# A hybrid streaming encoder layer: the top-k search of ten row tiles made in five pairs

## The chip, the core and the metric

The kernel runs on one core of one Trainium2 chip. The metric is the device time of one execution in microseconds (us). Five engines work from queues of their own, each in the order in which the program was written out: TensorE (PE for its matmuls, PEld for its weight loads), VectorE (DVE), ScalarE (ACT), GpSimd (POOL), and SyncE (SP), which issues nearly all DMAs.

## The reference, cut to what matters

One layer mixes three groups of heads: a gated delta rule with a short convolution (A), sparse attention (B) and attention over 256 memory tokens (C). All read one input projection `h @ w_in`. The change lies in group B, where an indexer scores every key for every query, and the keys of the 256 largest scores are kept:

```
adm = (k_pos[None, :] // CHUNK) <= (q_pos[:, None] // CHUNK)
logits = jnp.einsum('bqhd,bsd->bqhs', qi, ki)
score = jnp.einsum('bqh,bqhs->bqs', wi, jax.nn.relu(logits))
score = jnp.where(adm[None], score, -jnp.inf)
_, idx = lax.top_k(score, n_sel)        # n_sel = 256
```

There are 2048 prompt tokens (16 tiles of 128 rows, g = 1 to 16) and 128 sample tokens (tile 0, with 4112 keys each from a cache). Tile g of the prompt has 128 g keys, so tiles 1 and 2 keep all of them and tiles 3 to 16 search.

## The kernel before, in words

The kernel does not sort. For a tile of 128 queries it finds a threshold per row: `topk` takes mean and variance of a quarter of the scores (bn_stats on every fourth column), guesses the threshold T from a normal quantile, and corrects it in up to six counts (`NIT = 6`). A count is one pass of ScalarE over the scores, a sign with bias -T whose accumulator gives the number of keys above T; a chain of small instructions on VectorE then keeps the bracket (a lower and an upper point with their counts, in st4) and computes the next T. One pass of relu, fused multiply and max finds the scores next to the last T, the exact threshold is picked among them by rank, and a last pass writes a bias of 0 or -2**100 per key, which attention adds later. The count of the last pass must come out at 256: the square of its error is added to fail, and at the program's end a nonzero fail starts a slow exact selection.

In each small instruction of a search 128 rows of one tile lie on the partitions and one or two columns on the free axis: T, f (the count less 256), the masks, the bracket.

The program has two parts, each a set of generators that `weave` runs by modelled times: it takes the generator whose time is smallest, lets it issue one step and puts that step's modelled cost on its engine. What the engines run is the order that comes out of this and of the scheduler that follows it. In the first part (to about 1500 us) the generators are: the projections of five groups of row tiles (4, 4, 3, 3 and 3 tiles) with three matmuls per product of split operands (pp); their preparation; three stages of the delta rule (pa, pb, pl, po; GpSimd computes Lm for its block inverse, VectorE solves Xs step by step); and the index: memory keys, the sample tile, then `idx_prompt` for tiles 3 to 13 one after the other. Per tile, `idx_prompt` waits until the keys of the tile are projected (`done["i"] > g`), loads and splits the queries (`q_stack`: qr, qn, qst), computes 8 heads x ceil(W/512) matmuls into two PSUM buffers (pi), takes relu on ScalarE and adds the weighted result to score on VectorE, lets GpSimd set the masked corner of score, and runs `topk`. score has one buffer, so a tile's scoring starts when the search before is through. Tiles 14 to 16 follow in the second part (attention and output).

The names in rows: score is the tile of scores, junk the sign's output, tf holds f, T, f and -T, st is st4, msk the masks, tmp scratch, sg, thr and cnt the sign, threshold and counts, mv, sd, sdr, t_b the mean, the deviation and its inverse root. pp, pi, pa, pb, pl, po are PSUM tiles.

Weights come in by `load_w`, three raw pieces (wr) at a time, only in the first group; wh and wl are their split halves, kept in DRAM for the later groups.

Of the kernel before, what the change touches and what calls it, by code (L numbers as in the profile page):

```python
# [5 lines left out]
F32 = mybir.dt.float32  # L6
# [13 lines left out]
NT = 17  # L20
# [186 lines left out]
def build(tc, nc, a):  # L207
# [41 lines left out]
    fail = cpool.tile([128, 1], F32, name="fail")  # L249
# [207 lines left out]
    def idx_post(gi, t0, m, raw, sm, final):  # L457
# [3 lines left out]
        sq = spool.tile([128, 2, 32], F32, name="isq")  # L461
# [64 lines left out]
    def topk(pieces, get, put, g, tp):  # L526


        W = sum(w for _, w in pieces)
        ti = g - 2 if g else 15  # L530
        wst = 4096 if g == 0 else W - 128
        st = tp.tile([128, 8, 6], F32, name="bst")
        n = 0
        turn = [1]

        def order_():
            turn[0] = -turn[0]
            return range(len(pieces))[::-turn[0]]
        for i in order_():
            c0, w = pieces[i]  # L540
            s = yield from get(i)
            hi = min(w, wst - c0)
            for lo in range(0, hi, 2048):
                V.bn_stats(st[:, n, :], s[:, lo:min(lo + 2048, hi):4])
                n += 1
            put(i, -turn[0])
            yield 1
        mv = tp.tile([128, 2], F32, name="mv")
        V.bn_aggr(mv, st[:, :n, :])
        sd = tp.tile([128, 1], F32, name="sd")  # L550
        V.tensor_scalar(sd, mv[:, 1:2], 1e-30, None, op0=OP.add)
        rs = tp.tile([128, 1], F32, name="sdr")
        rsqrt(rs, sd, tp, "t")
        V.tensor_tensor(sd, sd, rs, op=OP.mult)
        zc = C("zc")[:, 2 * ti:2 * ti + 2]
        st4 = tp.tile([128, 4], F32, name="st4")
        V.scalar_tensor_tensor(st4[:, 0:1], sd, -4.0, mv[:, 0:1], op0=OP.mult, op1=OP.add)
        V.scalar_tensor_tensor(st4[:, 2:3], sd, 6.0, mv[:, 0:1], op0=OP.mult, op1=OP.add)
        V.memset(st4[:, 1:2], -float(NSEL))
        V.memset(st4[:, 3:4], float(W - NSEL))  # L560
        tf = tp.tile([128, 4], F32, name="tf")
        V.scalar_tensor_tensor(tf[:, 1:2], sd, zc[:, 0:1], mv[:, 0:1], op0=OP.mult, op1=OP.add)
        slope = tp.tile([128, 1], F32, name="slope")
        V.tensor_tensor(slope, sd, zc[:, 1:2], op=OP.mult)
        cnt = tp.tile([128, 4], F32, name="cnt")
        tmp = tp.tile([128, 4], F32, name="tmp4")
        msk = tp.tile([128, 4], I32, name="msk")

        def total():
            if len(pieces) > 1:  # L570
                V.tensor_reduce(cnt[:, 3:4], cnt[:, :len(pieces)], axis=AX.X, op=OP.add)
                return cnt[:, 3:4]
            return cnt[:, 0:1]

        def count():
            V.tensor_scalar(tf[:, 3:4], tf[:, 1:2], -1.0, None, op0=OP.mult)
            for i in order_():
# [3 lines left out]
                S.activation(jk[:, :w], s, AF.Sign, bias=tf[:, 3:4], accum_out=cnt[:, i:i + 1])  # L581
                put(i, -turn[0])
                yield 1
            V.tensor_scalar(tf[:, 0::2][:, :2], total().to_broadcast([128, 2]), 0.5, W / 2.0 - NSEL,
                            op0=OP.mult, op1=OP.add)
# [3 lines left out]
        for it in range(NIT):  # L589
            yield from count()  # L590
            if it == NIT - 1:
                break
            f, t_ = tf[:, 0:1], tf[:, 1:2]
            V.tensor_scalar(msk[:, 0:1], f, 0.0, None, op0=OP.is_gt)
            V.tensor_scalar(msk[:, 1:2], f, 0.0, None, op0=OP.is_le)
            V.copy_predicated(st4[:, 0:4:3], msk[:, 0:1].to_broadcast([128, 2]), tf[:, 1:3])
            V.copy_predicated(st4[:, 1:3], msk[:, 1:2].to_broadcast([128, 2]), tf[:, 0:2])
            V.tensor_tensor(tmp[:, 0:1], f, f, op=OP.mult)
            V.tensor_scalar(msk[:, 2:3], tmp[:, 0:1], 56.0 if it < 4 else 230.0, None, op0=OP.is_gt)
            if it == 0:  # L600
                V.scalar_tensor_tensor(tmp[:, 1:2], f, slope, t_, op0=OP.mult, op1=OP.add)
            else:
                V.tensor_tensor(tmp[:, 2:4], st4[:, 2:4], st4[:, 0:2], op=OP.subtract)
                V.reciprocal(tmp[:, 3:4], tmp[:, 3:4])
                V.scalar_tensor_tensor(tmp[:, 1:2], tmp[:, 3:4], st4[:, 3:4], tmp[:, 2:3], op0=OP.mult, op1=OP.mult)
                V.tensor_tensor(tmp[:, 1:2], tmp[:, 1:2], st4[:, 0:1], op=OP.add)
            V.copy_predicated(t_, msk[:, 2:3], tmp[:, 1:2])
            yield 1
# [26 lines left out]
        for i in range(3):  # L635
            if i:
                V.match_replace(tv, tops[:, 8 * i - 8:8 * i], tv, -3e38)
# [1315 lines left out]
```

## Time and profile before

| what | value |
|---|---|
| median of 3 runs | 2352.61 us (2351.39 to 2356.84) |
| profiled execution, its own time | 2355.36 us |
| its span, first to last instruction | 2353.5 us |
| mean granted TensorE clock | 0.946 |
| busy: TensorE, weight loads | 2096.8 us (89%), 1645.1 us (70%) |
| busy: VectorE, ScalarE, GpSimd | 1651.6 us (70%), 1292.9 us (55%), 419.7 us (18%) |

An engine's busy time counts its instructions alone; a matmul's end is modelled, so a busy TensorE can still be held up a little. A granted clock of 1 is 2.4 GHz, 0.5 is 1.2 GHz. Idle time in front of an instruction is put down to what it waited for last.

### The profile page before, as it was taken

The numbers are of one execution on the slowest core, as the hardware profiler recorded it, in microseconds if no ns is written. First come the engines' busy times: TensorE is split into PE (matmuls) and PEld (weight loads), VectorE is DVE, ScalarE is ACT, GpSimd is POOL, SyncE is SP. The second block draws the span as 40 slices with busy tenths as digits, with TensorE's granted clock in tenths as the row PEclk, the third lists the DMA queues.
The fourth block names the chain that finished last, engine by engine and source line by source line (L and its number), as shares of the span: only waits on it lengthen the run. The fifth ranks groups of instructions, "written<-read, shape, count | busy, mean of one in ns | idle before, by whom it ended". The sixth has DMA issues, their size and how long they took to land.

```text
span 2353.5 us, 43495 instructions
## 1 busy us (share of the span) xinstructions
PE 2096.8 (89%) x14123; PEld 1645.1 (70%) x14123; DVE 1651.6 (70%) x6571; ACT 1292.9 (55%) x3193; POOL 419.7 (18%) x494
## 2 busy tenths in 40 slices
PE   4887989788899998999899999989999999799997
PEld 3755645677688887888788888756566555467665
DVE  4765655566888787899888996777567667554552
ACT  3454545455546565676666764467456656544552
POOL 3231413211121111111111021132111111111100
PEclk9887989788999998999899999999999999999998
DMA  7688667765544555656555555368788777653212
GB/s 230 177 242 224 214 147 212 196 233 192 198 159 161 183 176 197 206 196 218 181 204 203 198 202 201 117 211 262 246 249 272 246 238 249 189 165 101 91 48 69
DMA packets 323533, 453.25 MB, mean 193 GB/s; under 512 B 81760, under 2 KB 230880, under 8 KB 303840
## 3 DMA queue, kind: packets, MB, share of 16 engines
q1 hardware_dynamic: 322976, 449.32, 59.9%
q8 instruction: 114, 1.87, 0.3%
q0 software_dynamic: 320, 1.06, 0.2%
q14 instruction: 123, 1.01, 0.1%
HBM read 344.53 MB, written 105.75 MB: 191 GB/s over the span
## 4 chain that ended last, share of the span: by engine, by line


## 5 line engine op out<-in xcount | busy, mean ns | idle before, releaser
L169 PE MATMUL pp<-wh,xh 128*128 128x256 f32 (+1 forms) x952 | 290.0, 305 | 10.6 <-ACT v L169 4.5
L169 PE MATMUL pp<-wh,xl 128*128 128x256 f32 (+1 forms) x952 | 280.6, 295 | 1.5 <-DVE xl L169 1.4
L169 PE MATMUL pp<-wl,xh 128*128 128x256 f32 (+1 forms) x952 | 280.5, 295 | 1.3 <-POOL wl L169 1.2
L169 PE MATMUL pp<-xh,wh 128*128 128x384 f32 (+1 forms) x640 | 249.5, 390 | 5.6 <-ACT q L169 3.2
L169 ACT ACTIVATE relu<-pi 128x512 f32<-128x512 f32 (+3 forms) x340 | 183.4, 545 | 125.0 <-PE pi L169 67.1
L169 PE MATMUL pp<-xh,wl 128*128 128x384 f32 (+1 forms) x640 | 242.2, 379 | 2.3 <-DMA wl<-wd2l 1.7
L169 DVE SCALAR_TENSOR_TENSOR score<-relu,w,score 128x512 f32<-128x512 f32 (+3 forms) x304 | 221.7, 731 | 29.5 <-ACT relu L169 15.0
L169 PE MATMUL pp<-xl,wh 128*128 128x384 f32 (+1 forms) x640 | 241.9, 378 | 0.0
L169 PEld LDWEIGHTS pp<-wh,xh 128*128 128x128 f32 x952 | 186.5, 196 | 17.6 <-ACT v L169 4.8
L169 PEld LDWEIGHTS pp<-wl,xh 128*128 128x128 f32 x952 | 186.3, 196 | 5.8 <-issue 2.5
L169 PEld LDWEIGHTS pp<-wh,xl 128*128 128x128 f32 x952 | 185.6, 195 | 5.1 <-DVE xl L169 2.7
L169 ACT ACTIVATE junk<-score,tf 128x1024 bf16<-128x1024 f32 (+11 forms) x126 | 142.5, 1131 | 69.8 <-DVE tf L169 47.9
L169 POOL TENSOR_TENSOR Lm<-Lp,cf 128x256 f32<-128x256 f32 (+1 forms) x120 | 85.0, 709 | 335.6 <-PE pb L169 312.2
L169 PE MATMUL pi<-kstack,qst 128*128 128x512 f32 (+3 forms) x304 | 129.6, 434 | 13.9 <-ACT relu L169 10.9
L169 PEld LDWEIGHTS pp<-xh,wh 128*128 128x128 f32 x640 | 125.4, 196 | 18.3 <-ACT q L169 3.8
L169 PEld LDWEIGHTS pp<-xh,wl 128*128 128x128 f32 x640 | 125.1, 196 | 15.6 <-issue 2.5
L169 PE MATMUL py<-woh,mixh 128*128 128x512 f32 x272 | 123.8, 455 | 11.6 <-ACT mixh L169 10.8
L169 PEld LDWEIGHTS pp<-xl,wh 128*128 128x128 f32 x640 | 125.4, 196 | 10.6 <-issue 2.5
L169 PE MATMUL py<-woh,mixl 128*128 128x512 f32 x272 | 111.4, 410 | 4.7 <-POOL mixl L169 4.5
L169 POOL TENSOR_TENSOR wl<-wr,wh 128x512 fp32r<-128x512 f32 (+1 forms) x61 | 80.7, 1333 | 188.8 <-ACT wh L169 186.3
L169 PE MATMUL py<-wol,mixh 128*128 128x512 f32 x272 | 110.6, 406 | 0.0
L169 ACT ACTIVATE PT<-pt 128x512 f32<-128x512 f32 (+1 forms) x112 | 64.3, 577 | 79.3 <-PE pt L169 78.4
(417 smaller groups left out, 5497.6 us busy)
## 6 DMA issues: line engine op xcount, KB each, us to landing
skt<-in_kT SPq DMA_DIRECT2D x128, 256.0 KB
svt<-in_v SPq DMA_DIRECT2D x128, 256.0 KB
nraw<-in_x SPq DMA_DIRECT2D x34, 256.0 KB
xres<-in_x SPq DMA_DIRECT2D x34, 256.0 KB
part_d<-xres SPq DMA_DIRECT2D x34, 256.0 KB
xres<-part_d SPq DMA_DIRECT2D x34, 256.0 KB
out_y<-xres SPq DMA_DIRECT2D x34, 256.0 KB
mixr<-mixT_d SPq DMA_DIRECT2D x33, 256.0 KB
```

The costliest lines, as they stand in the source:

```text
L169: return f(*args, **kw)
```

## The change

`topk` takes a list of tiles instead of one. For a list of two, each small tile gets a column per tile of the list (sh and small), so that one control instruction serves both. bn_stats, the sign passes, the relu and max passes and the last pass remain one per tile. The bracket st4 becomes low and upp, the row T, f, -T becomes cur. A constant that differs by tile (the number of keys) no longer fits an instruction's immediate: it lies in cst, low and upp, which GpSimd sets by memsets instead of VectorE. Where the scalar of a fused scalar_tensor_tensor differs by tile, the pair takes two tensor_tensor; a single tile keeps the fused one. The check has a column per tile in fail, and the two are added at the end.

`idx_prompt` takes lists: (3, 4), (5, 6), (7, 8), (9, 10), (11, 12) and (13,) in the first part, tiles 14 to 16 singly in the second. It waits for the keys of the list's last tile, scores all tiles of the list and then searches. The second tile's scores (score2) lie where the raw weights were: wr is now one tile of three slices, and score2 has its tag. isq goes from two buffers to one.

```diff
-    fail = cpool.tile([128, 1], F32, name="fail")
+    fail = cpool.tile([128, 2], F32, name="fail")
...
+    wraw = {"x": wpool.tile([128, WR, 512], F32, name="wr", bufs=1)}
+
     def load_w(src):
-        raw = wpool.tile(src.shape, F32, name="wr", bufs=WR)
+        n = int(np.prod(src.shape[1:]))
+        raw = wraw["x"][:, len(loaded) % WR, :n].rearrange("p (k c) -> p k c", k=src.shape[1])
         nc.sync.dma_start(raw, src)
...
+        def small(name, *n, dt=F32):
+            t = tp.tile([128, int(np.prod(n or (1,))), 2], dt, name=name)[:, :, :M_]
+            return t if n else t[:, 0]
...
+        cst = small("cst")
+        for m in range(M_):
+            G.memset(cst[:, m:m + 1], Ws[m] / 2.0 - NSEL)
...
-        V.memset(st4[:, 1:2], -float(NSEL))
-        V.memset(st4[:, 3:4], float(W - NSEL))
+        G.memset(upp[:, 1], -float(NSEL))
+        for m in range(M_):
+            G.memset(low[:, 1, m:m + 1], float(Ws[m] - NSEL))
...
+        def count(bias):
+            for m, (g, pieces, get, put) in enumerate(tiles_):
+                for i in order_(m):
+                    c0, w = pieces[i]
+                    s = yield from get(i)
+                    jk = tp.tile([128, JW], BF, name="junk")
+                    S.activation(jk[:, :w], s, AF.Sign, bias=bias[:, m:m + 1], accum_out=cnt[:, i + m:i + m + 1])
+                    put(i, -turn[0])
+                    yield 1
...
+        for it in range(NIT):
+            V.tensor_scalar(nT, T_, -1.0, None, op0=OP.mult)
+            yield from count(nT)
+            V.scalar_tensor_tensor(f, total(), 0.5, cst, op0=OP.mult, op1=OP.add)
...
+            V.tensor_scalar(msk[:, 0], f, 0.0, None, op0=OP.is_gt)
+            V.tensor_scalar(msk[:, 1], f, 0.0, None, op0=OP.is_le)
+            V.copy_predicated(low, msk[:, 0:1].to_broadcast(sh(2)), cur[:, 0:2])
+            V.copy_predicated(upp, msk[:, 1:2].to_broadcast(sh(2)), cur[:, 0:2])
+            new = tmp[:, 2]
+            V.tensor_tensor(new, f, f, op=OP.mult)
+            V.tensor_scalar(msk[:, 2], new, 56.0 if it < 4 else 230.0, None, op0=OP.is_gt)
...
+                V.tensor_tensor(tmp[:, 0:2], low, upp, op=OP.subtract)
+                V.reciprocal(tmp[:, 1], tmp[:, 1])
+                if M_ == 1:
+                    V.scalar_tensor_tensor(new, tmp[:, 1], low[:, 1], tmp[:, 0], op0=OP.mult, op1=OP.mult)
+                else:
+                    V.tensor_tensor(new, tmp[:, 1], low[:, 1], op=OP.mult)
+                    V.tensor_tensor(new, new, tmp[:, 0], op=OP.mult)
+                V.tensor_tensor(new, low[:, 0], new, op=OP.subtract)
+            V.copy_predicated(T_, msk[:, 2], new)
...
+        off = tmp[:, 1]
+        V.scalar_tensor_tensor(off, cst, 2.0, total(), op0=OP.mult, op1=OP.add)
+        V.tensor_scalar(off, off, 1.0, None, op0=OP.add)
+        V.tensor_tensor(off, off, off, op=OP.mult)
+        V.tensor_tensor(fail[:, :M_], fail[:, :M_], off, op=OP.add)
...
+    def idx_prompt(groups, tp, pl, top):
+        for gs in groups:
+            yield from until(lambda: done["i"] > gs[-1])
+            tiles_ = []
+            for x, g in enumerate(gs):
+                W = 128 * g
+                sc = wpool.tile([128, WR * 512], F32, name="score2", tag="wr", bufs=1) if x else tp.tile([128, top], F32, name="score")
...
+            yield from topk(tiles_, tp)
+            done["k"] = gs[-1]
...
-        yield from idx_prompt(range(3, EARLY), tp, pi, SLOT)
+        yield from idx_prompt([(g, g + 1) for g in range(3, EARLY - 1, 2)] + [(EARLY - 1,)], tp, pi, SLOT)
...
+        V.tensor_tensor(fail[:, 0:1], fail[:, 0:1], fail[:, 1:2], op=OP.add)
```

On VectorE, one correction of the threshold in the search of tile 5 (k, q and raw belong to the projections' convolution) before:

```order
L169 TENSOR_SCALAR tf<-cnt 128x2
L169 SCALAR_TENSOR_TENSOR q<-raw,cw,q 128x512
L169 TENSOR_SCALAR msk<-tf 128x1 x2
L169 TENSOR_TENSOR tmp_7820<-tf 128x1
L169 COPY_PREDICATED st_7810<-msk,tf 128x2 x2
L169 TENSOR_SCALAR msk<-tmp_7820 128x1
L169 TENSOR_TENSOR tmp_7820<-st_7810 128x2
L169 RECIPROCAL tmp_7820<-tmp_7820 128x1
L169 SCALAR_TENSOR_TENSOR q<-raw,q 128x512
L169 SCALAR_TENSOR_TENSOR tmp_7820<-tmp_7820,st_7810 128x1
L169 TENSOR_TENSOR tmp_7820<-tmp_7820,st_7810 128x1
L169 COPY_PREDICATED tf<-msk,tmp_7820 128x1
```

And the same correction in the search of the pair (5, 6) now:

```order
L169 SCALAR_TENSOR_TENSOR cur<-cnt,cst 128x2
L169 TENSOR_SCALAR msk<-cur 128x2 x2
L169 TENSOR_TENSOR tmp_7941<-cur 128x2
L169 COPY_PREDICATED low<-msk,cur 128x4
L169 COPY_PREDICATED upp<-msk,cur 128x4
L169 TENSOR_SCALAR msk<-tmp_7941 128x2
L169 TENSOR_TENSOR tmp_7941<-low,upp 128x4
L169 SCALAR_TENSOR_TENSOR Lp<-pa,dbp,e_8199 128x128
L169 RECIPROCAL tmp_7941<-tmp_7941 128x2
L169 TENSOR_TENSOR tmp_7941<-tmp_7941,low 128x2
L169 TENSOR_TENSOR tmp_7941<-tmp_7941 128x2
L169 TENSOR_TENSOR tmp_7941<-low,tmp_7941 128x2
```

One set of instructions with twice the columns stands where two sets stood, with one instruction more in it.

On GpSimd, the stretch ahead of the scoring of tile 4 (nth belongs to the norms, q and Lm to the delta rule, qn to `q_stack`) before:

```order
L169 TENSOR_TENSOR Lm<-Lp,cf 128x256
L169 TENSOR_TENSOR qn<-qr,qn 128x8x32
L169 TENSOR_TENSOR nth<-nraw,gains 128x512 x2
L169 MEMSET score 64x64
L169 TENSOR_TENSOR nth<-nraw,gains 128x512
L169 MEMSET Xs 32x256
L169 MEMSET Xs 32x16
L169 TENSOR_TENSOR Lm<-Lp,cf 128x256 x2
```

And the same stretch now, where the search of (3, 4) runs and (5, 6) is next:

```order
L169 TENSOR_TENSOR nth<-nraw,gains 128x512
L169 MEMSET upp 128x2
L169 TENSOR_TENSOR Lm<-Lp,cf 128x256
L169 MEMSET low 128x1 x2
L169 TENSOR_TENSOR Lm<-Lp,cf 128x256
L169 TENSOR_TENSOR nth<-nraw,gains 128x512 x2
L169 MEMSET cst 128x1 x2
L169 MEMSET Xs 32x256
L169 MEMSET Xs 32x16
L169 TENSOR_TENSOR Lm<-Lp,cf 128x256 x3
```

The memsets of the next pair stand among the delta rule's Lm, and the score memset with its qn is gone from here.

## Rows read from the trace of the kernel before

**Rows 1.** The page, busy time, share of the span and instructions of each engine.

```profile
PE 2096.8 (89%) x14123; PEld 1645.1 (70%) x14123; DVE 1651.6 (70%) x6571; ACT 1292.9 (55%) x3193; POOL 419.7 (18%) x494
```

**Rows 2.** The tile fail, 606 to 1414 us: duration min/median/max, first and last start.

```profile
L169 DVE TENSOR_TENSOR fail<-fail,cnt x11: 141/158/309, 652.1 to 1413.5; 128x1 f32<-128x1 f32 x11
```

**Rows 3.** Windows: length, then busy of PE, PEld, DVE, ACT, POOL, PEclk, DMA, GB/s.

```profile
606.00:1414.00 808.00, 746.32 (x4951) 679.25 (x4950) 709.35 (x3415) 502.65 (x1254) 120.16 (x180) 0.97 0.56 190
1414.00:1500.00 86.00, 84.43 (x578) 76.06 (x576) 58.82 (x236) 38.73 (x114) 11.78 (x21) 1.00 0.54 178
...
1050.00:1100.00 50.00, 49.64 (x328) 45.62 (x327) 48.22 (x214) 34.53 (x94) 4.18 (x8) 1.00 0.68 235
1100.00:1150.00 50.00, 39.56 (x240) 34.52 (x240) 47.46 (x276) 35.09 (x90) 9.06 (x12) 0.87 0.48 168
```

**Rows 4.** Waits of PE, 606 to 1414 us: total us, times, longest.

```profile
PE pi L169 <- POOL qn L169: 8.3, 2, 4.5
PE pi L169 <- ACT relu L169: 7.0, 9, 3.9
PE pl L169 <- DVE o L169: 6.7, 7, 2.8
...
PE pb L169 <- DMA Z<-blk: 3.7, 3, 1.9
...
PE pb L169 <- DVE tmp L169: 0.4, 1, 0.4
...
PE pl L169 <- ACT u L169: 0.2, 1, 0.2
```

**Rows 5.** Timeline of PE, 1130 to 1150 us: start, length, instruction, idle before.

```profile
1142.59 0.79 PE L169 MATMUL pi<-kstack,qst 128*128 128x512 f32 x1 [3.94 <-ACT relu L169]
```

**Rows 6.** The tile tf, 606 to 1414 us: durations in ns, min/median/max.

```profile
L169 DVE TENSOR_SCALAR msk<-tf x110: 130/144/156, 622.9 to 1390.5; 128x1 int32<-128x1 f32 x110
L169 DVE COPY_PREDICATED st<-msk,tf x110: 141/154/712, 623.6 to 1390.7; 128x2 f32<-128x2 int32 x110
...
L169 DVE TENSOR_SCALAR tf<-cnt x66: 147/168/937, 622.6 to 1394.8; 128x2 f32<-128x2 f32 x66
...
L169 DVE COPY_PREDICATED_SCALAR tf<-msk,tmp x55: 194/208/218, 624.4 to 1392.2; 128x1 f32 x55
...
L169 DVE TENSOR_SCALAR sg<-tf x11: 133/153/155, 640.3 to 1395.2; 128x1 f32<-128x1 f32 x11
```

**Rows 7.** The tile st, 606 to 1414 us.

```profile
L169 DVE MEMSET st<- x22: 59/59/59, 639.0 to 1392.5; 128x1 f32 x22
```

**Rows 8.** Timeline of DVE, 746 to 755 us.

```profile
748.17 0.19 DVE L169 TENSOR_SCALAR msk<-tf 128x1 int32<-128x1 f32 x2
748.30 0.14 DVE L169 TENSOR_TENSOR tmp<-tf 128x1 f32<-128x1 f32 x1
748.37 0.22 DVE L169 COPY_PREDICATED st<-msk,tf 128x2 f32<-128x2 int32 x2
748.51 0.13 DVE L169 TENSOR_SCALAR msk<-tmp 128x1 int32<-128x1 f32 x1
```

**Rows 9.** Waits of all engines, 606 to 1414 us.

```profile
POOL Lm L169 <- PE pb L169: 217.7, 63, 13.5
...
POOL score L169 <- DVE score L169: 65.7, 8, 20.9
...
POOL Xs L169 <- DMA blk<-Xs: 35.1, 4, 12.3
ACT junk L169 <- DVE tf L169: 31.1, 27, 2.8
```

**Rows 10.** Groups of DVE instructions, 606 to 1414 us: busy us, mean ns, idle before.

```profile
L169 DVE SCALAR_TENSOR_TENSOR score<-relu,w,score 128x512 f32<-128x512 f32 (+3 forms) x208 | 145.0, 699 | 21.5 <-ACT relu L169 10.8 <-DMA score<-in_epsrow 9.3 <-issue 0.3
```

**Rows 11.** The tile score on POOL, 606 to 1414 us.

```profile
L169 POOL MEMSET score<- x11: 148/149/153, 616.6 to 1365.4; 64x64 f32 x11
```

**Rows 12.** The tile fail, the whole span.

```profile
L169 DVE TENSOR_TENSOR fail<-fail,cnt x15: 141/153/309, 604.8 to 2045.0; 128x1 f32<-128x1 f32 x15
```

More of the change, by code (lines that the diff above doesn't have):

```diff
@@ L460, in idx_post @@
         k3 = sm[:, :m, 0:32]
-        sq = spool.tile([128, 2, 32], F32, name="isq")
+        sq = spool.tile([128, 2, 32], F32, name="isq", bufs=1)
         V.tensor_tensor(sq[:, :m], k3, k3, op=OP.mult)
@@ L524, in q_stack @@
         return qst
[L526 to L532, printed above, removed]
-        n = 0
[L534 to L558, printed above, removed]
-        V.memset(st4[:, 1:2], -float(NSEL))
-        V.memset(st4[:, 3:4], float(W - NSEL))
[L561 to L577, printed above, removed]
@@ L583, in count @@
                 yield 1
-            V.tensor_scalar(tf[:, 0::2][:, :2], total().to_broadcast([128, 2]), 0.5, W / 2.0 - NSEL,
-                            op0=OP.mult, op1=OP.add)
-        NIT = 6
-        yield 1
[L589 to L608, printed above, removed]
@@ L660, in topk @@
-        V.tensor_scalar(cnt[:, 0:1], total(), float(W - 2 * NSEL + 1), None, op0=OP.add)
-        V.tensor_tensor(cnt[:, 0:1], cnt[:, 0:1], cnt[:, 0:1], op=OP.mult)
-        V.tensor_tensor(fail, fail, cnt[:, 0:1], op=OP.add)
-        yield 1
-    def idx_prompt(gs, tp, pl, top):
-        for g in gs:
-            W = 128 * g
-            yield from until(lambda: done["i"] > g)
-            sc = tp.tile([128, top], F32, name="score")
-            nc.sync.dma_start(sc[:, :W], a["epsrow"][:, :W].to_broadcast([128, W]))
-            qst = yield from q_stack(g, tp, pl)
-            for c in range(0, W, 512):
-                n = min(512, W - c)
-                for h in range(8):
-                    ps = pl.tile([128, 512], F32, name=pl.name)
-                    T.matmul(ps[:, :n], qst[:, h, :], kstack[:, c:c + n], start=True, stop=True)
-                    r = tp.tile([128, 512], F32, name="relu", bufs=2)
-                    S.activation(r[:, :n], ps[:, :n], AF.Relu)
-                    yield 1
-                    V.scalar_tensor_tensor(sc[:, c:c + n], r[:, :n], w8[:, g, h:h + 1], sc[:, c:c + n],
-                                           op0=OP.mult, op1=OP.add)
-            G.memset(sc[0:64, W - 64:W], MASKED)
-            nc.sync.dma_start(score_d[g, :, :W], sc[:, :W])
-            cuts = [(0, W)] if W <= JW else [(0, 1024), (1024, W - 1024)]
-            def resident(i):
-                return sc[:, cuts[i][0]:sum(cuts[i])]
-                yield
-            yield from topk(cuts, resident, lambda i, up: None, g, tp)
-            done["k"] = g
@@ L785, in idx_sample @@
         fetch(1)
[L786 removed]
+        yield from topk([(0, cuts, reload, put)], tp)
     def memory_keys(tp, px):
@@ L1676, in late @@
                 if first:
-                    yield from idx_prompt(range(EARLY, NT), tp, pi, SLOT)
+                    yield from idx_prompt([(g,) for g in range(EARLY, NT)], tp, pi, SLOT)
             def more():
@@ L1910, in build @@
     with tc.tile_pool(name="flag", bufs=1) as fp, tc.tile_pool(name="fps", bufs=1, space=PSUM) as fps:
+        V.tensor_tensor(fail[:, 0:1], fail[:, 0:1], fail[:, 1:2], op=OP.add)
         pf = fps.tile([1, 1], F32, name="pf")
-        T.matmul(pf, fail, C("one")[:, 0:1], start=True, stop=True)
+        T.matmul(pf, fail[:, 0:1], C("one")[:, 0:1], start=True, stop=True)
         ok = fp.tile([1, 1], I32, name="ok")
```

189 lines of the change are left out of this document (138 added, 51 removed).

## The prediction

> **What bounds the kernel now.** I read the views from wide to narrow. The page says that TensorE is busy 89% of the span and VectorE 70% [rows 1], an average over two programs that run one after the other. The search of tiles 3 to 13 lies in the first: the last instruction of a search, the update of fail, comes 11 times between 652.1 and 1413.5 us [rows 2]. So the stage to read is 606 to 1414 us, and the table of windows shows it beside the stretch behind it, 1414 to 1500, in which the projections run on and no search does [rows 3]. The reader is to see two things there. In the stage VectorE is busy 709.35 of 808 us, 88%, nearly as much as TensorE with 746.32, 92%. And TensorE stands idle for 61.7 us, 7.6%, at a granted clock of 0.97; in the stretch without a search it is idle 1.6 of 86 us, 1.8%, at 1.00. The list of what TensorE waited for [rows 4] puts 26.9 us of the 61.7 down to VectorE (16 rows), 21.0 to ScalarE (9 rows), 8.3 to GpSimd and 3.7 to a DMA. Those waits are what a lighter VectorE can give back; the end of the program itself is set by TensorE's work, of which the change touches nothing. The waits bunch where one group of row tiles gives way to the next: from 1100 to 1150 us TensorE is busy 39.56 of 50 us while VectorE is at 47.46, and the granted clock is 0.87 [rows 3]; inside it lies the longest single wait, 3.94 us [rows 5].
>
> **The change part by part.** *Pairs.* A search of one tile has 93 control instructions on VectorE: two memsets and 91 others, on 1 or 2 columns (counted in the code; the counts of its forms, 110, 66, 55 and 11 for 11 tiles, stand in [rows 6]). A pair has 99 for its two tiles: one set instead of two, but each of the seven fused scalar_tensor_tensor whose scalar differs by tile becomes two tensor_tensor, and the check at the end has one more. So 2 x 93 - 99 = 87 go per pair, 435 for five pairs, of which 20 are memsets of 59 ns [rows 7]. What one costs lies between two numbers. Its median duration is 0.144 to 0.208 us [rows 6], so 435 x 0.15 = 65 us from above. But durations overlap: where independent ones follow each other, the starts are 0.06 to 0.07 us apart (748.17, two of msk, 748.30, 748.37) [rows 8], so 435 x 0.065 = 28 us from below. In the same rows a dependent one starts 0.13 us or more behind its input and other streams fill the gap; I take 45 us, in the middle. Instructions on [128,2] and [128,4] instead of [128,1] and [128,2] I cost at nothing: the forms of one and of two columns have medians of 0.144 and 0.154 [rows 6].
>
> How much of 45 us reaches TensorE? Not all: most of VectorE's work lies beside matmuls. VectorE's idle time in the stage goes from 98.65 to about 144 us of 808. If what queues in front of it goes as busy over idle, that falls from 709/99 = 7.2 to 664/144 = 4.6, by 36%; if it goes as busy time alone, by 6%. On the 26.9 us that is 9.7 or 1.7 us. The same chain also holds up ScalarE: its sign counts waited 31.1 us in 27 places for the new threshold [rows 9]. Ten of eleven chains become five, so some 14 us of that go, though a count then passes over two tiles. ScalarE is busy 502.65 of 808 us [rows 3], so most of this vanishes in its slack; of the 21.0 us that TensorE waited for ScalarE I take a tenth, 2.1. The clock gives something back where waits shorten. A mean of 0.97 over 808 us is up to 24 us of lost speed; but it is lost where TensorE idles at a change of groups (0.87 from 1100 to 1150, 1.00 in the 50 us before) [rows 3], and those changes stay, so I take 1. Against it stand the new waits below, 2. Sum: 9.7 + 2.1 + 1 - 2 = 10.8, and as the 36% is the larger of its two ends I round down to 10 us.
>
> *Order.* The scoring of both tiles of a pair now comes before either search: 145.0 us of VectorE in the stage, unchanged in amount [rows 10]. Pairs must wait for the keys of the later tile, but the order of the matmuls shows no loss by it: tile 13's last scoring matmul moves from behind 4162 of the 4793 projection matmuls to behind 4007. At the stage's 4951 matmuls in 808 us [rows 3] these 155 are 25 us, and more with the other matmuls between them: the searches end earlier. What follows, the end of the projections up to 1500 us, is TensorE at 84.43 of 86 us [rows 3] and gains nothing by an early search.
>
> *Memsets to GpSimd.* The constants are set by GpSimd, in 40 memsets, 25 of them for the pairs. Each takes about what the score memset does there, 0.149 us [rows 11], 6 us in all on an engine that is busy 120.16 of 808 [rows 3]. The cost is in the wait: the order puts upp, low and cst of the next pair ahead of Lm, and they may be written only when VectorE has last read those of the pair before. The one comparable wait of before, the score memset for VectorE's score, took 65.7 us in 8 places [rows 9], TensorE's waits for GpSimd being 8.3 us in 2 places in all [rows 4]. From below it costs 0, since Lm and q wait for TensorE longer (217.7 us in 63 places) [rows 9]; from above, 12 waits (two for each of five pairs and tile 13) of 8.3 / 2 = 4.15 us each, 50 us. I take 2, near the lower end, because in the order qn or Xs and not Lm follows the cst memsets of four pairs of five, and Xs itself waited for a DMA of its own (35.1 us in 4 places) [rows 9].
>
> *The rest.* The raw weights as slices of one tile: the same loads with the same waits in SP's and GpSimd's order, up to the first pair nothing moves on TensorE; 0. isq with one buffer: read and written on VectorE alone; 0. One addition more at the end: the last search writes fail at 2045.0 us [rows 12], 300 us before the span ends; under 0.2 us. Tiles 0 and 13 to 16 alone: two memsets less and one instruction more each; 0.
>
> The profiled execution took 2355.36 us (span 2353.5, 1.9 around it); the sum gives 2345.4 against it. The median of the runs is 2352.61, 2.75 lower, so the forecast for a median is 2342.6, say 2343 us.
>
> **The rivals.** *TensorE paces the stage and nothing changes.* For it: from 1050 to 1100 us VectorE is at 48.22 of 50 and TensorE still at 49.64 [rows 3], so a full VectorE alone does not stop it. Against it: the idle share of 7.6% beside 1.8%. Time: the 6% end, 1.7 us, less the 2 of the memsets: 2353.
>
> *VectorE is the bound, and all it sheds is gained.* Then the 28 to 65 us come back in full up to what there is, 808 x (7.6% - 1.8%) = 47 us. For it: 88% busy over 808 us and the window at 1100. Against it: the window at 1050. Time at the lower price: 2352.6 - 28 = 2325. The Trainium skill (Perfetto Trace Analysis, Identifying the Most-Contended Engine) has the engine with the highest occupancy as the one to optimise first, and judges TensorE by its weight loads rather than by its matmuls. By that rule, with weight loads at 679.25 us against 709.35, VectorE would be this stage's engine and 2325 the time; the window at 1050 speaks against it, that at 1100 for it.
>
> *GpSimd's memsets hold up the inverse.* The memset of upp or cst stands in GpSimd's queue until VectorE is through with the last pair; Lm, q and qn behind it come late, and TensorE's pb matmuls wait for Lm. For it: the score memsets did wait, 8.2 us on average, and the wait for cst ends only with the very last instruction of the pair before. Against it: only 8.3 us of TensorE's idle time came from GpSimd. It decides from the third wait of 12 that reaches TensorE: 3 x 4.15 = 12.5 us eat the gain. With half of them, 25 us: 2352.6 - 12.8 + 25 = 2365, slower.
>
> **How the numbers follow.** Chances: the forecast 0.45, nothing 0.22, the full gain 0.12, the memsets 0.21. A measurement of this kernel tells about 0.2% from no change, 4.7 us. The forecast and the full gain count as faster: 0.57. Same: 0.22. Slower: 0.21. With 28 us of VectorE's time instead of 45 the 36% becomes 25%, with 65 it becomes 45%, and the sum 7.8 or 13.2: the likeliest case's own range is 2339 to 2346. The range for 8 in 10 goes from 2326, where most of the full gain begins, to 2363, where half of the rival with the memsets is left out.
>
> **What would show it.** Right: in the stage VectorE has some 435 instructions less and 30 to 60 us less busy time, while TensorE's waits for VectorE fall from 26.9 to under 20; the searches end 25 us or more before 1413.5; from 1100 to 1150 TensorE is busier than 39.56. ScalarE's wait for the threshold falls by nearly half from 31.1. Wrong: TensorE's waits for GpSimd grow beyond 8.3, with upp, low or cst as what GpSimd waited at (the memsets); the idle share stays at 7.6% with VectorE lighter (TensorE paces); or the time moves outside the stage, behind 1500 us, where I expect the same spacing as before.

## The result, and the profile after

The changed kernel takes 2369.55 us in the median of 13 runs (2358.82 to 2377.9), the kernel before 2355.29 beside it; the ratio is 1.0058, 95% interval 1.0036 to 1.0079. It is slower, and the forecast of 2343 us was wrong. A second set of runs (e5 below) gave 1.0057, 1.0037 to 1.0076. The profiled execution of the changed kernel took 2363.54 us, its span is 2361.7. It lies 6 us under the median of its kernel, while the profiled execution of before, 2355.36, lies at its own, so the two profiles show 8.2 us of a loss of some 14.

The windows of [rows 3], of the changed kernel now (length, then busy of PE, PEld, DVE, ACT, POOL, granted clock, DMA share, GB/s):

```profile
606.00:1414.00 808.00, 752.90 (x4983) 682.91 (x4982) 685.78 (x3002) 507.07 (x1272) 123.39 (x211) 0.97 0.56 192
1414.00:1500.00 86.00, 84.76 (x578) 77.15 (x579) 57.13 (x227) 36.76 (x106) 11.61 (x20) 1.00 0.48 162
1050.00:1100.00 50.00, 46.05 (x306) 42.92 (x305) 46.34 (x267) 37.87 (x94) 6.12 (x13) 0.97 0.56 193
1100.00:1150.00 50.00, 40.47 (x228) 34.90 (x227) 47.16 (x173) 33.71 (x87) 7.60 (x11) 0.90 0.62 208
```

VectorE has 413 instructions and 23.6 us less than in [rows 3], and TensorE is busy 6.6 us more. The last search of the first program ends at 1371.6 us, 42 us earlier than in [rows 2]. The last projection matmul starts at 1505.99 instead of 1509.68 us. So up to there the change has gained some 4 us; the 8.2 us by which the span is longer arise behind 1500 us, where nothing was changed but the code of three single searches. What lies there, first before and then after:

```profile
1500.00:1600.00 100.00, 83.10 (x564) 55.75 (x565) 76.63 (x285) 59.83 (x170) 31.95 (x35) 0.91 0.60 188
```

```profile
1500.00:1600.00 100.00, 82.75 (x536) 52.21 (x535) 71.80 (x290) 56.77 (x155) 25.23 (x31) 0.84 0.63 195
```

TensorE is busy nearly as long, but has done 28 matmuls less, at a granted clock of 0.84 instead of 0.91. The place is found with two lines of the timelines, the last projection matmul (pp) on PE and the end of the last head's triangular inverse on VectorE, the copy Zs<-Xs; before:

```profile
1509.68 0.28 PE L169 MATMUL pp<-wh,xl 128*128 128x256 f32 x1
...
1514.24 0.36 DVE L169 COPY Zs<-Xs 24x256 f32<-24x256 f32 x1
```

and after:

```profile
1505.99 0.28 PE L169 MATMUL pp<-wh,xl 128*128 128x256 f32 x1
...
1534.29 0.35 DVE L169 COPY Zs<-Xs 24x256 f32<-24x256 f32 x1
```

Before, the inverse (30 dependent VectorE instructions behind a round trip through DRAM) is done 4.6 us behind the last projection matmul; after, 28.3 us behind it, in the middle of tile 14's scoring and of the other work with which the second program begins. The order says the same: the last (k,k) matmul of that head, from which the inverse is made, stands behind 4723 of the 4793 projection matmuls before and behind 4770 after, and 8 and 19 score additions of tile 14 stand ahead of that copy on VectorE. In the changed kernel the windows there are:

```profile
1506.00:1526.00 20.00, 14.56 (x79) 9.63 (x77) 17.53 (x69) 10.95 (x34) 5.81 (x7) 0.91 0.61 183
1526.00:1546.00 20.00, 15.07 (x87) 7.92 (x86) 18.42 (x52) 11.23 (x28) 6.49 (x6) 0.64 0.60 179
```

From 1526 to 1546 VectorE is busy 18.42 of 20 us, TensorE has 5 us idle and does the rest at a clock of 0.64, that is for most of the time at the lower level (1.2 GHz), behind 20 us in which it had been idle a quarter of the time. In the kernel before the like 20 us hold 126 matmuls, here 87:

```profile
1530.00:1550.00 20.00, 17.21 (x126) 11.45 (x126) 17.28 (x39) 13.06 (x38) 9.23 (x9) 0.91 0.67 204
```

There, too, the 20 us ahead had held TensorE busy for only 15.08 us (1510 to 1530 us, granted clock 0.83), so the idle quarter alone does not tell the two apart. TensorE's longest waits from 1506 to 1546 us, in the changed kernel, are two of 2.8 us each, for the delta rule's Z and o on VectorE.

### The profile page after: what moved, and what is told of

Read it like the earlier page. It is cut to its first block, busy times and chain, and to the rows that moved or that the text cites. A ratio compares the mean times of both kernels' runs of the same rounds, so it can differ in the third digit from the quotient of the medians.

```text
span 2361.7 us, 43110 instructions
## 1 busy us (share of the span) xinstructions
PE 2104.9 (89%) x14123; PEld 1648.6 (70%) x14123; DVE 1618.2 (69%) x6132; ACT 1293.4 (55%) x3193; POOL 419.8 (18%) x534
## 4 chain that ended last, share of the span: by engine, by line
PE 54%; DVE 18%; DMA 10%; ACT 5%; issue 3%; POOL 1%; SPq 0%; DVEq 0%; ACTq 0%; POOLq 0%
PE pp L169 15%; PE py L169 13%; PE po L169 5%; PE pi L169 5%; PE pt L169 5%; PE pb L169 5%; PE ps L169 3%; DVE score L169 2%; PE pl L169 2%; DMA svt<-in_v 2%; PE pa L169 2%; ACT junk L169 2%; DMA skt<-in_kT 1%; DMA wr<-in_w_n 1%; DVE xt L169 1%
## 5 line engine op out<-in xcount | busy, mean ns | idle before, releaser
L169 DVE SCALAR_TENSOR_TENSOR score<-relu,w,score 128x512 f32<-128x512 f32 (+3 forms) x304 | 214.2, 705 | 28.5 <-ACT relu L169 19.7
L169 ACT ACTIVATE junk<-score,cur 128x1024 bf16<-128x1024 f32 (+8 forms) x126 | 142.3, 1130 | 42.6 <-DVE cur L169 34.8
L169 PE MATMUL pi<-kstack,qst 128*128 128x512 f32 (+3 forms) x304 | 134.8, 454 | 13.9 <-ACT relu L169 11.5
```

What stands on the lines that cost most here:

```text
L169: return f(*args, **kw)
```

## The experiments

All were timed in five rounds beside the kernel before, and each left one profile. From every profile three stretches were read by counting matmuls in TensorE's timeline: S1 from the 1401st to the last projection matmul (pp), S2 from there to the 41st po<-PT matmul of the second program, S3 from there to the last py matmul with mixh or mixl. Inv is the start of the last Zs<-Xs less that of the last projection matmul. All in us; the interval behind a ratio is in the text. The theories T1 to T12 are named in the expectations, each where it first comes up.

| kernel | ratio | S1 | S2 | S3 | Inv |
|---|---|---|---|---|---|
| before | 1 | 903.1 | 135.6 | 699.7 | 4.6 |
| after | 1.0058 | 896.5 | 145.5 | 701.9 | 28.3 |
| e5 after again | 1.0057 | 901.8 | 141.2 | 711.6 | 28.1 |
| e1 old late | 0.9993 | 896.7 | 148.5 | 694.4 | 28.0 |
| e2 no pairs | 1.0007 | 897.2 | 134.2 | 705.4 | 4.6 |
| e3 layout | 0.9997 | 904.1 | 138.0 | 700.8 | 4.6 |
| e4 memsets on VectorE | 1.0025 | 902.3 | 140.9 | 713.6 | 29.0 |
| e6 pairs, other order | 1.0003 | 909.3 | 131.0 | 698.8 | 3.8 |
| e7 tile 14 early | 0.9938 | 913.3 | 132.2 | 674.9 | 10.8 |
| e8 before, other order | 1.0034 | 900.0 | 140.8 | 698.2 | 22.3 |
| e9 more control | 1.0064 | 909.2 | 145.2 | 693.1 | 24.1 |
| e10 three passes | 0.9955 | 891.4 | 133.5 | 708.0 | 3.0 |
| e11 before, early 15 | 1.0022 | 904.5 | 159.3 | 681.4 | 44.4 |
| e12 pairs, early 16 | 0.9967 | 916.8 | 147.0 | 661.0 | 15.4 |
| e13 inverse early | 0.9990 | 899.2 | 129.7 | 702.8 | 2.1 |
| e14 fewer control | 0.9955 | 896.5 | 135.2 | 709.4 | 2.7 |
| e15 narrow counts | 0.9979 | 890.8 | 149.0 | 694.6 | 33.5 |
| e16 pairs, third order | 1.0032 | 904.0 | 133.2 | 705.3 | 4.6 |

The same kernel moves from execution to execution: after and e5 are one program and differ by 5 in S1 and 10 in S3. Before and e3, which have one order, differ by 1 in both. And a profile can be of an unusual execution: those of e4, e10 and e14 are of the slowest in their sets, 14, 12 and 11 us above the median, that of e8 is of the fastest, 14 us below. So the sum of a row need not show what the ratio shows; S2, which differs by 4 between after and e5, is the steadier sign.

**e1, old late.** Tiles 14 to 16 are searched by the code of before:

```diff
-                    yield from idx_prompt([(g,) for g in range(EARLY, NT)], tp, pi, SLOT)
+                    yield from idx_prompt1(range(EARLY, NT), tp, pi, SLOT)
```

> The changed kernel, but row tiles 14 to 16, whose search lies in the second program, are searched by the code of before; pairs, memsets on GpSimd for them, and the raw weights as one tile stay. T1 (the pairs gain a few us in the first program, and the loss comes from the second, because the new search code for its three single tiles changes the order that the planner writes there): the first program still ends near 1506 us, as in the changed kernel, the second takes 832 to 841 us from there to the last py matmul, as before (835), and not 847; median 2346 to 2356, ratio to before 0.996 to 1.000. T2 (the layout: one tile for the raw weights, one buffer for isq, makes the start of the second program late): still 847 us, ratio 1.004 or more. T3 (GpSimd's memsets of the pairs hold up the first program): nothing of it is taken away, ratio 1.004 or more. T4 (the pairs themselves leave a worse rest for the second program): ratio 1.004 or more.

0.9993 (0.9972 to 1.0014): the loss is gone with all pairs still there, so T3 and T4 fall as they were put, and the place in the second program holds. But it did not go as T1 had it: the inverse stays late (28.0) and S2 long, and S3 is 7 us and more shorter. One order was exchanged for another.

**e2, no pairs.** All tiles singly in the new code:

```diff
-        yield from idx_prompt([(g, g + 1) for g in range(3, EARLY - 1, 2)] + [(EARLY - 1,)], tp, pi, SLOT)
+        yield from idx_prompt([(g,) for g in range(3, EARLY)], tp, pi, SLOT)
```

> The changed kernel without pairs: row tiles 3 to 13 one by one in the new search code, with its memsets on GpSimd. T1: the first program ends as before or later (1508 to 1512 us in the trace), the second is as slow as in the changed kernel (843 to 850 us after it): median 2360 to 2370, ratio 1.003 to 1.006. T2: the same. T3: 11 searches instead of 6 have the memsets, the first program ends at 1515 or later, ratio above 1.006. T4: the loss goes with the pairs, 2352 to 2357, ratio 0.999 to 1.001.

1.0007 (0.9992 to 1.0022), with the inverse in its old place: T1 falls in the form it had, since the new code for the single tiles alone costs nothing. The ratio is the one that T4 gave; only e1 speaks against T4.

**e3, layout.** The raw weights as one tile, isq with one buffer and fail with two columns, in the kernel before (cut to the first):

```diff
-        raw = wpool.tile(src.shape, F32, name="wr", bufs=WR)
+        raw = wraw["x"][:, len(loaded) % WR, :n].rearrange("p (k c) -> p k c", k=src.shape[1])
```

> The kernel before with three edits alone: the raw weights as slices of one tile, one buffer for isq, two columns for fail. Every engine has the instructions of before in the order of before. T2 (the layout costs the loss): ratio 1.004 or more, first matmul po of the second program's first tile 10 us or more later than before (1589). T1, T3, T4: ratio 0.999 to 1.001.

0.9997 (0.9981 to 1.0013): T2 falls.

**e4, memsets on VectorE.**

```diff
-            G.memset(cst[:, m:m + 1], Ws[m] / 2.0 - NSEL)
+            V.memset(cst[:, m:m + 1], Ws[m] / 2.0 - NSEL)
...
-        G.memset(upp[:, 1], -float(NSEL))
+        V.memset(upp[:, 1], -float(NSEL))
```

> The changed kernel with its 40 constants set by VectorE instead of GpSimd. T3 (GpSimd waits 82 us in 6 places at cst in the changed kernel's stage 606 to 1414, and what is queued behind holds TensorE up): the waits go, the first program ends at 1500 us or earlier instead of 1506, ratio to before 0.999 or less. T1: TensorE waited for GpSimd only 3.5 us there, so the first program's end moves by less than 3 us; the order of the second program is written anew by the planner, so its length may be anything between 832 and 850 us, and the ratio 0.997 to 1.007. T2 and T4: ratio 1.004 or more.

1.0025 (1.0007 to 1.0043). S1 is not shorter without GpSimd's waits for the constants, so T3 falls; the time, lower than that of the changed kernel, comes with yet another order, in which S2 is still long.

**e5, after again.** No edit.

> The changed kernel as it is, a second profile and a second set of runs beside the others. All theories: median 2362 to 2374, ratio to before 1.004 to 1.008. From the last projection matmul to the 41st po<-PT matmul of the second program some 146 us as in the first profile (before: 136), with the last inverse (the last copy Zs<-Xs on VectorE) 28 us behind the last projection matmul (before: 4.6).

1.0057 (1.0037 to 1.0076); S2 141.2 where 146 was expected, Inv as expected.

By then Inv and S2 went together, and T5 was formed: the loss is the late inverse. The planner's pause ahead of the last pass of a search changes the order and no operation, which gave the next two.

**e6, pairs in another order.** In topk:

```diff
-        yield 3000.0
+        yield 1000.0
```

> The changed kernel with one number of the planner changed: the pause ahead of the last pass of a search is 1000 and not 3000. The operations are the same; their order is written anew, and in it the last (k,k) matmul of the heads stands behind 4722 of the 4793 projection matmuls, as in the kernel before (4723), and not behind 4770. T5 (the loss is that last head's inverse, which in the changed kernel comes late and lies among the scoring of tile 14 at the start of the second program): the last inverse ends within 10 us of the last projection matmul, the stretch to the 41st po<-PT matmul takes 134 to 139 us again instead of 146, and the median falls by 7 us or more under that of the changed kernel (ratio to before below 1.003). T6 (pairing costs, by whatever way, in any order): ratio to before 1.004 or more. T7 (every new order draws another time, by more than what the pairs do): any ratio from 0.997 to 1.007.

1.0003 (0.9985 to 1.0021), the inverse 3.8 us behind, S2 131.0, 3 us below the stretch that T5 gave. T5 holds, T6 falls; T7's wide range holds it, too.

**e7, tile 14 early.**

```diff
-EARLY = 14
+EARLY = 15
...
-        yield from idx_prompt([(g, g + 1) for g in range(3, EARLY - 1, 2)] + [(EARLY - 1,)], tp, pi, SLOT)
+        yield from idx_prompt([(g, g + 1) for g in range(3, 13, 2)] + [(g,) for g in range(13, EARLY)], tp, pi, SLOT)
```

> The changed kernel, but tile 14, too, is searched in the first program, behind tile 13, where the changed kernel leaves VectorE idle (2.6 of the last 10 us busy), so that its scoring no longer lies at the start of the second. T5: the stretch from the last projection matmul to the 41st po<-PT matmul falls to 136 us or less, ratio to before 0.994 to 1.000. T6: ratio above 1.002. T7: the first program loses as much as the second gains, or not, by its order: 0.995 to 1.005.

2340.1 us, 0.9938 (0.9917 to 0.9959): faster than both kernels, just below T5's and T7's ranges. S1 is 10 us longer than before, S3 25 us shorter. Tile 14's search lies in the stretch that had room; compare VectorE here with 57.13 above:

```profile
1414.00:1500.00 86.00, 79.83 (x551) 74.31 (x550) 74.25 (x372) 50.78 (x135) 13.90 (x26) 1.00 0.57 198
```

**e8, before in another order.** The same pause at 6000 in the kernel before.

> The kernel before with the same number of the planner changed, 6000 instead of 3000: the same operations, no pairs, but the last (k,k) matmul of the heads behind 4758 of the 4793 projection matmuls instead of 4723. T5: the last inverse ends 15 us or more behind the last projection matmul, the start of the second program takes 143 us or more, ratio to before 1.003 or more. T6: 0.998 to 1.002, as nothing is paired. T7: anything from 0.997 to 1.007, without a bond to the place of the inverse.

1.0034 (1.0018 to 1.0051), Inv 22.3, S2 140.8: no pair in it, and more than half of the loss. S2 is 2 us less than T5 asked for. Its profile is of an execution 14 us faster than the median, so the loss itself can't be placed in it.

**e9, more control.**

```diff
             V.copy_predicated(t_, msk[:, 2:3], tmp[:, 1:2])
+            for _ in range(8 if 0 < g < EARLY else 0):
+                nc.vector.tensor_scalar(t_, t_, 1.0, None, op0=OP.mult)
```

> The kernel before with 8 more VectorE instructions of one column in each of five passes of the searches of tiles 3 to 13, on the path to the new threshold: 440 instructions, about as many as the pairs take away, and 28 to 66 us of VectorE by the durations of such instructions. T8 (VectorE's load in the first program bounds TensorE there, so what the pairs shed should have been worth 8 to 28 us): from the 1401st to the last projection matmul it takes 8 us or more longer than before (903), and the ratio to before is 1.004 or more. T9 (TensorE paces the first program at either load, and differences of some us there are the order's): 895 to 910 us, as in all kernels so far.

1.0064 (1.0041 to 1.0086). The ratio is T8's. S1 is 6 us longer, 2 less than T8 asked for and inside T9's range, and the inverse came late, which has its own price, so this run does not decide. TensorE's waits for VectorE from 606 to 1414 us sum to 35.3 us (before 26.9).

**e10, three passes.**

```diff
-        NIT = 6
+        NIT = 3 if 0 < g < EARLY else 6
```

> The kernel before, but the search of tiles 3 to 13 makes 3 of its 6 passes and leaves out the check at its end, so that the thresholds of these tiles are not the exact ones: some 430 VectorE instructions and 39 to 50 sign counts of ScalarE less in the first program, much as the pairs take away and without pairs. T8: the first program's stretch falls by 8 us or more under 903, ratio 0.996 or less. T9: 895 to 910 us, ratio 0.997 to 1.003.

0.9955 (0.9939 to 0.9971), S1 891.4: T8, not T9. A lighter search does help the first program; whether by VectorE's instructions or ScalarE's counts, both of which it drops, this run can't say.

**e11, before with tile 14 early.** EARLY = 15 in the kernel before.

> The kernel before, without pairs, with tile 14 searched in the first program. If the pairs made the room for it (T10): the first program, whose searches end 42 us later without pairs, cannot take tile 14 in its last 100 us, its last inverse comes late, and the ratio to before is 0.999 or more, against 0.994 with pairs. If it is the move of tile 14 alone (T11): 0.992 to 0.997, as with pairs.

1.0022 (1.0003 to 1.0040): T10. In this order, without pairs, tile 14's search ends at 1511.2 us instead of 1484.8, the inverse comes 44.4 us late and S2 takes 159.3.

**e12, tile 15 early too.** EARLY = 16 in e7.

> The changed kernel with tiles 13, 14 and 15 searched in the first program, one by one behind the five pairs. If the first program still has room (VectorE 57 of 86 us busy behind 1414 us in the changed kernel): under 2340, ratio below 0.994. If tile 14 has filled it: the search of tile 15 runs beyond the last projection matmul and TensorE waits there, ratio 0.995 or more.

0.9967 (0.9948 to 0.9986), 0.3% behind e7, though the intervals touch: tile 15's search ends at 1584.3 us, 59 us behind the last projection matmul.

**e13, inverse early.** The changed kernel; (4, 2) is the third head of the last group:

```diff
         R.update(Lp=Lp, at=at, X=X, Z=Z, cc=cc, nbe=nbe, rq=rq)
-        yield 6000.0
+        yield 2000.0 if (gi, h) == (4, 2) else 6000.0
```

> The changed kernel with one pause of the planner shorter: behind the third head of the last group, 2000 instead of 6000. TensorE's order is that of the changed kernel up to the last 250 of the 4793 projection matmuls; the last (k,k) matmul then stands behind 4723 of them instead of 4770. T5 (the late last inverse costs it): the last inverse ends within 12 us of the last projection matmul instead of 28 behind it, the stretch to the 41st po<-PT matmul takes 131 to 138 us (changed kernel: 141 and 146), ratio to before 1.003 or less, from 1.0057. T7 (that place goes along with slow orders, and another part of the second program's order costs the time): the stretch may shorten, the ratio stays at 1.004 or more.

2350.73 us, 0.9990 (0.9968 to 1.0013). The same 100 us as above:

```profile
1500.00:1600.00 100.00, 85.54 (x631) 56.16 (x631) 76.34 (x302) 64.65 (x184) 30.76 (x34) 0.95 0.66 205
```

and the copy, behind a last projection matmul at 1506.91:

```profile
1509.01 0.37 DVE L169 COPY Zs<-Xs 24x256 f32<-24x256 f32 x1
```

One pause for one head takes the whole loss away: 631 matmuls instead of 536 in these 100 us, S2 12 to 16 us shorter, 16 us in the ratio. So T5 holds here and T7, which asked for 1.004 or more, does not. The pause also writes what follows in a new order; which part of the gain is the early inverse itself and which that order, no run splits.

**e14, fewer control.** In the kernel before:

```diff
+            if 0 < g < EARLY:
+                V.scalar_tensor_tensor(tmp[:, 1:2], f, slope, t_, op0=OP.mult, op1=OP.add)
+                V.tensor_copy(t_, tmp[:, 1:2])
+                yield 1
+                continue
```

> The kernel before, single tiles, with the bracket of the search taken out for tiles 3 to 13: each pass steps by the slope alone, some 460 VectorE instructions less, all sign counts of ScalarE as before; the check at the end of these tiles is left out, and their thresholds are not the exact ones. T8 (VectorE's instructions in the search hold up TensorE): from the 1401st to the last projection matmul 895 us or less, from 903. T9 (TensorE paces, and the rest is order): 896 to 910. T12 (ScalarE's counts are what counts): the same, 896 to 910.

0.9955 (0.9934 to 0.9977). S1, 896.5, misses T8's bound by 1.5 and lies in the range of T9 and T12. TensorE's waits for VectorE do fall, from 26.9 to 17.3 us in the stage, with the largest at

```profile
PE pl L169 <- DVE o L169: 4.9, 6, 1.5
...
PE pb L169 <- DVE Z L169: 2.2, 5, 0.8
```

while VectorE is as busy as in the changed kernel (685.78 above):

```profile
606.00:1414.00 808.00, 755.67 (x5005) 687.41 (x5004) 686.58 (x2973) 509.01 (x1277) 121.41 (x186) 0.96 0.56 191
```

Where the 10 us of the ratio lie, the profile of this long execution can't show: S1, S2 and S3 together are 3 us longer than before's. And it is one order.

**e15, narrow counts.** The six sign passes over 64 columns, in the kernel before.

> The kernel before with the sign counts of the six passes over 64 columns instead of the tile's width, for tiles 3 to 13: VectorE's instructions as before, some 60 us less of ScalarE in the first program; thresholds not the exact ones, the check at the end of these tiles left out. T12 (the 12 us of the three passes came from ScalarE's shorter counts): the stretch takes 895 us or less. T8 and T9: 896 to 910.

0.9979 (0.9961 to 0.9998) in spite of an inverse 33.5 us late; S1 890.8: T12. By S1, ScalarE's counts weigh as much as VectorE's instructions or more (12 us here, 7 in e14); again it is one order and one profile each.

**e16, a third order.** The pause at 8000 in the changed kernel.

> The changed kernel with the planner's pause ahead of the last pass of a search at 8000: the same operations in a third order, the last (k,k) matmul behind 4723 projection matmuls, 8 score additions of tile 14 ahead of the last inverse's end (before 8, changed kernel 19). T5: start of the second program 131 to 138 us, ratio 1.003 or less. T9: the first program's stretch 895 to 910 us. T6 (pairing costs in any order): ratio 1.004 or more.

1.0032 (1.0010 to 1.0054) with the inverse early and S2 133.2. T5's ratio is missed by 0.0002 and its stretch met: the slowness of this order lies elsewhere, and I don't know where. So an early inverse alone does not make an order fast, and by e1 a late one alone need not make it slow.

Over all 18 profiles: where Inv is 10.8 or less (nine), S2 is 129.7 to 138.0; where it is 15.4 or more (nine), 140.8 to 159.3. The two groups do not overlap, though S2 is not the same work in every order: between its ends lie 876 (e4) to 991 (e11) matmuls, 900 to 905 in before, after and e5.

## Why the prediction was wrong

**The step that failed** is the sentence that behind 1500 us the same spacing was to be expected, with the zero for tiles 0 and 13 to 16. It costed the code there and not its order. The pairs change the modelled times in the first program; the last head's stage then starts some us later against the projections, and what is 47 projection matmuls in TensorE's order is 24 us on VectorE. S2 is 12 to 16 us shorter without it (e13), and it is not the pairs' own: other orders of the pairs do not have it (e6), and an order without pairs has it (e8). It could have been read before the run, from the order of the changed kernel where the programs meet.

The traces show how the inverse got so late. Its first instruction starts 3.9 us behind the last projection matmul instead of 8.5 ahead of it, and from there to the copy Zs<-Xs it takes 24.4 us instead of 13.1. Between its instructions VectorE runs 54 others of 20.3 us, before 16 of 6.0 us; tile 14's score additions are only 4.4 us of that. More comes from small instructions that end together with a wide one of GpSimd, which in the changed kernel splits output weights (wol) just then; the last instruction of the inverse is one of them (GpSimd's first):

```profile
1532.85 1.29 POOL L169 TENSOR_TENSOR wol<-xres,woh 128x512 fp32r<-128x512 f32 x1 [2.53 <-ACT woh L169]
1532.93 1.23 DVE L169 TENSOR_TENSOR Xs<-Xs,xt 24x15 f32<-24x15 f32 x1
```

The same form took 0.17 us at the start of the inverse before. Seven small instructions end so inside these 24.4 us, together 6.4 us beyond 0.16 us each; before it was one, with 0.5 us, and wol came only behind the inverse, at 1516.8.

And what S2 pays is mostly not waiting. S2 as a window, of before, after and e13:

```profile
1509.68:1645.30 135.62, 117.51 (x902) 76.16 (x902) 104.82 (x394) 89.18 (x250) 37.81 (x38) 0.94 0.70 223
```

```profile
1505.99:1651.50 145.51, 126.39 (x909) 80.26 (x908) 104.79 (x410) 88.53 (x251) 36.91 (x42) 0.88 0.71 221
```

```profile
1506.91:1636.60 129.69, 114.49 (x887) 72.38 (x887) 97.39 (x381) 86.02 (x240) 35.01 (x39) 0.96 0.74 227
```

TensorE is idle 18.1, 19.1 and 15.2 us: 1 of the 9.9 us between before and after, 4 of the 15.8 between e13 and after. The rest is busy time, on 7 and 22 matmuls more, at a granted clock of 0.88 instead of 0.94 and 0.96. The timed runs agree: their mean granted clock is 0.939 for the changed kernel (13 runs) and 0.942 in e5 (6), but 0.946 for the kernel before (26, beside e5) and 0.944 for e13 (12). That the late inverse brings the clock down is argued from this going together, not shown by itself.

S2 is also not the whole loss. Of the 13.5 us by which the span of e5 is longer than that of before, 5.7 lie in S2 and 11.9 in S3, with the order of the changed kernel; why S3 moves so between executions stays open.

**The 9.7 us from VectorE's backlog** did not come either. Seven profiles with the five pairs and tile 14 left late (after, e1, e4, e5, e6, e13, e16) have S1 of 901.4 in the mean, four of the single full search (before, e2, e3, e8) 901.1. The load fell by 23.6 us, not 45: even the lower bound of 28 was too high, since 413 instructions took away 0.057 us each, a little less than the distance of starts in [rows 8]. But the wait is the real miss. The sum of TensorE's waits for VectorE, 26.9 us in [rows 4], is now 27.1, and 26.9 to 28.6 in e5, e6, e13 and e16 (the 6.6 us that TensorE is busier come from elsewhere: GpSimd and a DMA, 8.3 and 3.7 us before, hold it up for 3.5 us and not at all now):

```profile
PE pl L169 <- DVE o L169: 7.8, 10, 2.4
PE pb L169 <- DVE Z L169: 7.7, 11, 1.3
```

So the rule of busy over idle failed as well, and not only the 45 us put into it. For the 23 us that really went it gives 21%, a fall from 26.9 to some 21. At the same load of VectorE the pairs have 27.1 (685.78 us busy) and e14, which keeps single tiles, 17.3 (686.58); that these 17.3 are 36% less, the figure worked out for 45 us, is chance. So the load alone does not set the wait; it matters how the instructions go. With pairs the waits only move: by stretches of 100 us they fall from 9.0 to 2.8 between 700 and 900 us and rise from 2.8 to 6.3 between 606 and 700 and from 0.4 to 4.3 between 1000 and 1100; that is where TensorE, at 49.64 of 50 us in [rows 3] from 1050 to 1100, is now at 46.05. Two tiles' scorings stand back to back (31.1 us of score additions between 950 and 1050, 17.7 before). That this is the cause is argued, not shown; no run took the scorings apart.

**ScalarE.** Its waits for the threshold fell from 31.1 us in 27 places [rows 9] to 22.0 in 18, less than forecast, and TensorE's waits for ScalarE did not fall by 2.1: they went from 21.0 to 22.8. e15 speaks for a share of ScalarE in S1.

**The clock**: 0.97 in the stage as before; 0.90 instead of 0.87 from 1100 to 1150, where TensorE is at 40.47, a little over 39.56, as said. The 1 us can't be told apart. Behind 1500 us, where the sum had no term for it, the clock fell, as S2 shows.

**The memsets.** GpSimd did wait where the rival had it wait, at cst 13.6 us each time and at upp 1.6, where the rival had 4.15 for either:

```profile
POOL cst L169 <- DVE tmp L169: 81.7, 6, 30.4
...
POOL upp L169 <- DVE tmp L169: 9.4, 6, 2.7
```

Yet TensorE's waits for GpSimd fell from 8.3 to 3.5 us, and S1 did not gain without these memsets (e4). The cover named in the prediction held: Lm waits for TensorE 171.1 us in the stage. No run tells the 2 us from nothing; the rival's time, 2365, came near the measured one by luck, as the mechanism was another.

**The rest.** The searches ended 42 us earlier (25 or more expected), and up to 1500 us this gained nothing, as said: TensorE at 84.76 of 86. The layout is worth nothing (e3). The likeliest case's own range should have ended at 2345, which is what 7.8 us gives, and not at 2346. The rival that TensorE paces the stage had the right size for what this change does in it, but as a reason it does not fit e10 and e15, where S1 is 12 us shorter. By its rule to optimise the engine with the highest occupancy first, and to judge TensorE by MFU (the share of its peak rate, not worked out here) and weight loads, the Trainium skill (Perfetto Trace Analysis, Identifying the Most-Contended Engine) would have worked on VectorE here, busy 709.35 us beside 679.25 of weight loads. The pairs, which relieve VectorE by 23.6 us, do not agree with it; e14, which relieves it by 22.8, does by its ratio of 0.9955, in one order.

## What to carry to other kernels

Where a planner writes the order, every edit draws a new one: orders of the same operations differed here by 0.3 to 0.7%, more than the edit was worth, so compare a change in several orders, and read its order at the seams between programs, where a long dependent chain can fall among the next program's work. Work that an engine sheds is worth what the engine behind it stops waiting, and that has to be measured as a wait; here 23 us less left TensorE's waits at 27 us in one form and at 17 in the other. The room it leaves can be worth more than the work: filled with the next tile's search it gave 0.6% (e7). A stretch that grows without more waiting may have lost clock: compare its busy time, its matmuls and its granted clock.

## What was unexpected of the hardware

Small VectorE instructions sometimes take eight times as long. The addition of two columns of fail, forecast under 0.2 us, took 1.24:

```profile
L169 DVE TENSOR_TENSOR fail<-fail,tmp x10: 141/150/1117, 609.0 to 2050.6; 128x1 f32<-128x1 f32 x5, 128x2 f32<-128x2 f32 x5
...
L169 DVE TENSOR_TENSOR fail<-fail x1: 1240/1240/1240, 2053.0 to 2053.0; 128x1 f32<-128x1 f32 x1
```

The same form has 141 ns at its shortest. What the slow ones share can be read from the trace: GpSimd ran a wide instruction beside both (mixl<-mixr,mixh, 128x512, from 1884.69 and from 2052.72 us), and each addition ended 0.01 to 0.02 us behind its end. In this profile 62 of the 64 VectorE instructions that read and write 1 to 4 columns of 128 partitions and took more than 0.6 us ended within 0.04 us of the end of a GpSimd instruction, in all 18 profiles 1258 of 1282. No run here moved GpSimd's wide work away to see them shorten.
